# A hybrid attention layer on one core: the query norms of ten heads applied in full, key squares summed in one matmul, and a pair's sums issued at other steps

## The chip, the cores and the metric

The kernel runs on one core of a Trainium2 chip. The metric is device time in microseconds for one execution. A core has a tensor engine (PE, with its weight loads shown apart as PEld), a vector engine (DVE), a scalar engine (ACT), GpSimd (POOL) and a sync engine (SP) that issues DMAs. Each engine works through its own queue in order; semaphores hold an instruction until what it reads is there.

## The reference

One layer of a decoder trunk on 512 tokens of 2048 numbers. After an RMS norm, one wide projection gives queries, keys and values of two groups of heads. Eight forgetting heads (FoX) attend causally with a learned decay. Eight NSA query heads share two key groups and attend to compressed, selected and windowed keys. Queries and keys are RMS-normalised per head (QK-norm), which is what the change is about. An output projection, a residual add, and a gated feed-forward layer follow. Cut to what matters here:

```python
def _rms_norm(x, g):
    xf = x.astype(jnp.float32)
    y = xf * lax.rsqrt(jnp.mean(xf * xf, axis=-1, keepdims=True) + RMS_EPS)
    return (y * g.astype(jnp.float32)).astype(x.dtype)

proj = h @ w_in
qf, kf, vf, ff, qn, kc, vc, ks, vs, kw, vw, gt = jnp.split(proj, cuts, axis=-1)
qf = _rms_norm(qf.reshape(B, T, Hf, Dh), fox_q_norm)
kf = _rms_norm(kf.reshape(B, T, Hf, Dh), fox_k_norm)
qn = _rms_norm(qn.reshape(B, T, G, R, Dh), nsa_q_norm)
```

## The kernel before

[...] All matmuls are done in parts: a 32-bit operand is split into a high part (a copy by ACT that rounds) and a low part (what is left, by DVE), and three products of parts stand for one. `split2` (lines 208 to 216) does this for activations, `split_w` (236) for weight tiles `wp`, of which there are two buffers.

The program has these stretches. Up to 60 us a first projection runs. From 60 to 440 the rest of the plain projections is woven with the eight NSA heads and forgetting head 0. From 440 to about 652 six `pair` projections (query and key of forgetting heads 2 to 7 together) and two `vpair` projections run as a form with seven products in place of eight, each product 24 matmuls of 256 columns. Then the output projection, gate and up, and down follow; the change doesn't touch them.

What sets the order: `stagger` (269) runs the projections one after another; each yields `POST` when its matmuls are done, and what is left of it (the norm) is then advanced as "late steps", one at every second step of the next projection from step 7 on (step 4 in the pair stretch, `LAG7`). `weave` (285) puts the attention of the heads between these steps; in the pair stretch `attend` (1149) does so by the table `SPANS`. On top of this a scheduler orders each engine's instructions, so the built order counts more than the written one.

There are two ways to normalise a query or key before the change:

- `normed` (471) is for keys. It scales the projection by the token's factor `rstd` on DVE (`scaled`, 389), squares it in two halves, adds them, splits the sum's 64 rows into `fr`, and forms the sums with one matmul, `ones` as weights and `fr` moving (484), so that every partition holds every token's sum. Then `rsqrt` (319) and one `scalar_tensor_tensor` (488) give the normalised tile, which is split into two parts.
- `query` (454) is for queries. It splits the raw projection times the gain at once, and forms the sums as columns, one number for each token, with four small matmuls in which `fr` is the weight and `ones[:, :2]` moves (`square_sums`, 423, the matmul on 431). `factors` (434) makes a factor `qs` of each row of the scores, and its inverse, in eight small ops. The head's scores are then multiplied by `qs` on DVE as they leave PSUM (604), its biases `nb` are divided by it on POOL (822, 851), and its compressed scores are scaled by it on ACT (607).

In a `pair` (1087) the query goes the second way: squares of the query (1095), one late step; then the key's squares (1098), the copies `fr_q` (inside `square_sums`), a late step, the sums `ss_q` (431) and the copies of the key's squares, two full tiles `fr`; a late step; the key's sums `ss_k` with two matmuls (1105); a late step; the factors, the key's norm and its split.

`fox(h)` (843) is a forgetting head: scores, softmax, four scalings of p on ACT (617), transposes pT on PE (633), their split (`pt`), and products with the values. `nsa(h)` (815) is an NSA head.

Of the kernel before, what the change touches and what calls it, by code (L numbers as in the profile page):

```python
# [12 lines left out]
OP = mybir.AluOpType  # L13
# [70 lines left out]
def hybrid_layer(ctx: ExitStack, tc: tile.TileContext, xT, vec, ffb, wfg, wfirst, win, cmpw, wout, wos, wgu, wdn, out):  # L84
# [279 lines left out]

    gains = ap_.tile([P, 6], F32, name="gains")
    nc.vector.tensor_scalar_mul(gains, vt[:, 0:6], -0.5 / HD)
    for i in (V_FQ, V_NQ):
        nc.vector.tensor_scalar_mul(gains[:, i:i + 1], vt[:, i:i + 1], -SCALE)
# [84 lines left out]

    def query(name, gain, kept):

        z = yield from proj(name, True)
        r = place()
        if kept:
            t = ftile(f"t_{name}")
            nc.scalar.activation(t, z, AF.Copy, scale=gain)  # L460
        else:
            split2(r, z, gain)
        sq = squares(name, z)
        yield POST
        o = yield from square_sums(name, sq, "m")
        if kept:
            split2(r, t)
        yield
        live[name] = r, *factors(name, o)

    def normed(name, gain, tag, bufs=5):
# [16 lines left out]
        nc.vector.scalar_tensor_tensor(t, t, gain, y, op0=OP.mult, op1=OP.mult)  # L488
        if tag == "ox":
            r = [loose(f"{name}{p}") for p in range(2)]  # L490
        else:
            r = ap_.tile([P, KV], FR, tag=tag, name=name, bufs=bufs)
            if name[:2] == "ks":
                with_compressed[name] = r[:, :64 + T]
                if name == "ks1":
                    nc.scalar.activation(r[:, :64], Kc1.bitcast(F32), AF.Copy)
            r = r[:, 64:64 + 2 * T].rearrange("p (s t) -> p s t", s=2)

            first_keys[name] = r[:, :, :P]
            r = [r[:, p] for p in range(2)]  # L500
# [63 lines left out]
    class Branch:  # L564


        def __init__(self, name, q, k, v, nbs, gcol, apart=False, first_keys=None):
            self.kc = None
            q, self.qs, _ = q
            self.name, self.q, self.k, self.v, self.nbs, self.gcol, self.apart = name, q, k, v, nbs, gcol, apart  # L570
            self.first_keys = first_keys

        def scores(self):
# [3 lines left out]
            for i in reversed(range(NB)):  # L577
# [20 lines left out]
                else:  # L598
# [4 lines left out]
                    nb = pi  # L603
                nc.vector.tensor_tensor_reduce(pi, s[:, :n], nb, self.qs[:, i:i + 1], 3e38, OP.add, OP.min, st[:, 0, i:i + 1])
                if self.kc is not None and i < NB - 1:
                    for n, at in ((i, 0), (NB - 1, 64 + P))[:1 + (i == 0)]:
                        nc.scalar.activation(self.into[:, n, :64], b[:, at:at + 64], AF.Copy, scale=self.qs[:, n:n + 1])
                nc.scalar.activation(pi, pi, AF.Exp, scale=-1.0, bias=st[:, 0, i:i + 1], accum_out=st[:, 1, i:i + 1])
# [206 lines left out]
    def nsa(h):  # L815
        g = h // 4
        q = live.pop(f"qn{h}")

        def nbs(i):
            n = P * (i + 1)  # L820
            nb = ap_.tile([P, T], F32, tag="nb", name=f"nb{h}{i}", bufs=2)
            nc.gpsimd.tensor_scalar(nb[:, :n], E[:, T - n:], q[2][:, i:i + 1], 2.0 ** -(h + 1), op0=OP.mult, op1=OP.mult)
            return nb[:, :n]

        o = ps.tile([P, T], F32, tag="o", name=f"on{h}")
        s, w = [Branch(f"{b}{h}", q, live[f"k{m}{g}"], live[f"v{m}{g}"],
                       nbs, 3 * h + c, b == "w", first_keys.get(f"k{m}{g}"))
                for b, m, c in (("s", "s", 1), ("w", "w", 2))]
# [14 lines left out]
    def fox(h):  # L843
# [4 lines left out]
        def nbs(i):  # L848
            n = P * (i + 1)
            nb = ap_.tile([P, T], F32, tag="nb", name=f"nbf{h}{i}", bufs=2)  # L850
            nc.gpsimd.tensor_scalar(nb[:, :n], ck[:, :n], ncq[:, i, h:h + 1], q[2][:, i:i + 1], op0=OP.add, op1=OP.mult)
            nc.gpsimd.affine_select(nb[:, n - P:n], nb[:, n - P:n], pattern=[[-1, P]], compare_op=OP.is_ge,
                                    fill=BIG, base=0, channel_multiplier=1)
            return nb[:, :n]
# [19 lines left out]
    def nsa_q(h):  # L874
        return query(f"qn{h}", gain(V_NQ), h < 2)

# [210 lines left out]
    def pair(h):  # L1087
# [8 lines left out]
        yield  # L1096
        ks = ftile(f"sq_{k}")
        nc.scalar.activation(ks, t, AF.Square)
        oq = yield from square_sums(q, sq, "t", 2)
        fr = [ap_.tile([P, T], FR, tag=tag, name=f"fr_{k}{tag}") for tag in ("fr", "sb")]  # L1100
        split2(fr, ks)
        yield
        ok = ps.tile([P, T], F32, tag="t", name=f"ss_{k}", bufs=2)
        for p in range(2):
            nc.tensor.matmul(ok, ones, fr[p], start=(p == 0), stop=(p == 1))
        yield
# [928 lines left out]
```

## Time and profile before

| What | us |
|---|---|
| Median of three runs | 2093.97 (2092.68 to 2099.3) |
| The profiled execution | 2096.57 |
| Its span on the core | 2094.8 |

| Stretch of the span, us | PE idle, us | What runs |
|---|---|---|
| 0 to 60 | 1.1 | first projection |
| 60 to 440 | 3.9 | projections, NSA heads, forgetting heads 0 and 1 |
| 440 to 660 | 15.0 | pairs, forgetting heads |
| 660 to 832 | 2.8 | output projection |
| 832 to 2095 | 4.6 | gate, up, down |

The idle times are a stretch's length less PE's busy time in it. PE is busy nearly throughout, and a busy PE need not be at full speed: the granted clock is a column of its own. Two views read alike but differ: the table of waits names the engine whose instruction ended last before PE went on, while the timeline rows of that engine tell what that instruction had waited for itself.

### The profile page before, as it was taken

How to read it: one execution, taken by the hardware profiler on the slowest of the kernel's cores; microseconds unless marked ns; L12 is line 12 of the kernel's file. 1: busy time of each engine (PE TensorE's matmuls, PEld its weight loads, DVE VectorE, ACT ScalarE, POOL GpSimd, SP SyncE). 2: the span in 40 equal slices, each digit the busy share in tenths (PEclk: the TensorE clock that was granted, in tenths of full speed). 3: DMA queues.
4: the chain of work that ended last, by engine and by line, in shares of the span. 5: the costliest groups of instructions: out<-in, count | busy, mean ns of one | idle time of the engine just before them, and what ended most of it. 6: DMA issues, size and time to landing. Idle time of an engine off the chain costs nothing.

```text
span 2094.8 us, 40209 instructions
## 1 busy us (share of the span) xinstructions
PE 2067.6 (99%) x16219; PEld 1984.4 (95%) x16219; DVE 1785.5 (85%) x2738; ACT 1069.1 (51%) x1420; POOL 360.8 (17%) x545
## 2 busy tenths in 40 slices
PE   9999999999999999999999999999999999999999
PEld 8888988899998898999999999999999999999999
DVE  6677678887777877999999999999999987889898
ACT  6556565666666545534444343343433455565554
POOL 1043454522121011111111111111111000000000
PEclk9999999999999999999999999999999999999999
DMA  5685776966675575576776777777777797579865
GB/s 210 207 181 164 177 169 176 217 199 177 208 184 181 177 250 180 165 209 184 195 191 189 204 184 181 209 183 197 193 185 202 239 332 260 153 237 329 299 176 150
DMA packets 142155, 424.24 MB, mean 203 GB/s; under 512 B 17608, under 2 KB 17608, under 8 KB 141968
## 3 DMA queue, kind: packets, MB, share of 16 engines
q1 hardware_dynamic: 91168, 289.21, 41.4%
q0 software_dynamic: 44176, 106.19, 25.8%
q10 hardware_dynamic: 6624, 26.27, 3.3%
q8 instruction: 127, 2.08, 0.4%
q14 instruction: 60, 0.49, 0.1%
HBM read 389.34 MB, written 124.53 MB: 245 GB/s over the span
## 4 chain that ended last, share of the span: by engine, by line
PE 88%; DVE 5%; ACT 3%; issue 2%; DMA 1%; POOL 0%; DVEq 0%; ACTq 0%; SPq 0%; POOLq 0%
PE q L1780 40%; PE pd L1919 13%; PE pd L1924 7%; PE ps_kf L1061 3%; PE po L1370 2%; PE ps_vs L544 2%; PE ps_qn L259 1%; PE po L261 1%; PE ps_vf L544 1%; PE ps_qn L261 1%; PE ps_qn L260 1%; PE po L259 1%; PE po L260 1%; PE ps_vf L1061 1%; PE ps_first L261 1%
## 5 line engine op out<-in xcount | busy, mean ns | idle before, releaser
L95 ACT ACTIVATE bigm<-r 128x1792 fp32r<-128x1792 f32 x174 | 298.2, 1714 | 454.6 <-PE q L1780 320.0
L92 DVE TENSOR_TENSOR bigm<-r,bigm 128x1792 fp32r<-128x1792 f32 x174 | 351.4, 2019 | 5.8 <-ACT bigm L95 5.2
L92 DVE TENSOR_TENSOR r<-r 128x512 f32<-128x512 f32 x522 | 267.2, 512 | 34.5 <-DMA r<-wgu 22.3
L141 POOL DMA_DIRECT2D wsum<-wdn x176 | 120.4, 691 | 700.9 <-ACT bigm L95 602.8
L1780 PE MATMUL q<-bigm 128*128 128x256 f32 x1848 | 217.0, 276 | 0.0
L1780 PE MATMUL q<-formy,bigm 128*128 128x256 f32 x1848 | 216.8, 276 | 0.0
L1780 PE MATMUL q<-forma,bigm 128*128 128x256 f32 x1848 | 216.8, 276 | 0.0
L1780 PE MATMUL q<-formx,bigm 128*128 128x256 f32 x1848 | 216.8, 276 | 0.0
L1780 PEld LDWEIGHTS q<-bigm 128*128 128x128 f32 x1848 | 213.1, 188 | 0.0
L1780 PEld LDWEIGHTS q<-forma,bigm 128*128 128x128 f32 x1848 | 213.0, 188 | 0.1
L1780 PEld LDWEIGHTS q<-formy,bigm 128*128 128x128 f32 x1848 | 212.9, 188 | 0.1
L1780 PEld LDWEIGHTS q<-formx,bigm 128*128 128x128 f32 x1848 | 212.9, 188 | 0.0
L1919 PE MATMUL pd<-bigm 128*128 128x256 f32 x1200 | 146.9, 276 | 0.0
L1919 PEld LDWEIGHTS pd<-bigm 128*128 128x128 f32 x1200 | 141.0, 188 | 0.0
L92 DVE TENSOR_TENSOR bigm<-wd,bigm 128x1024 fp32r<-128x1024 f32 (+1 forms) x62 | 107.8, 1738 | 12.5 <-ACT bigm L95 12.3
L95 ACT ACTIVATE bigm<-rawm 128x768 fp32r<-128x768 f32 (+2 forms) x72 | 66.0, 927 | 98.9 <-PE pd L1924 64.3
L95 ACT ACTIVATE bigm<-wd 128x1024 fp32r<-128x1024 f32 (+1 forms) x62 | 91.1, 1469 | 9.8 <-DVE wd L92 6.1
L92 DVE TENSOR_TENSOR bigm<-rawm,bigm 128x768 fp32r<-128x768 f32 (+2 forms) x72 | 75.5, 1058 | 23.8 <-ACT bigm L95 23.0
L1924 PE MATMUL pd<-bigm 128*128 128x256 f32 x600 | 80.7, 276 | 0.0
L1061 PE MATMUL ps_kf<-bigm,wp_kf 128*128 128x256 f32 x576 | 79.7, 290 | 0.3 <-DVE wp_kf L92 0.3
L1061 PEld LDWEIGHTS ps_kf<-bigm,wp_kf 128*128 128x128 f32 x576 | 74.6, 197 | 1.1 <-DVE wp_kf L92 0.5
L141 POOL DMA_DIRECT2D fsump<-win x72 | 49.1, 751 | 150.6 <-ACT wp_ks L95 39.5
(626 smaller groups left out, 4373.4 us busy)
## 6 DMA issues: line engine op xcount, KB each, us to landing
r<-wgu SPq DMA_DIRECT2D x174, 512.0 KB, 4.3
wsum<-wdn POOLq DMA_DIRECT2D x176, 256.0 KB, 5.1
rawm<-ad SPq DMA_DIRECT2D x44, 512.0 KB, 6.7
wd<-wdn SPq DMA_DIRECT2D x40, 512.0 KB, 6.0
wd<-wsum SPq DMA_DIRECT2D x40, 512.0 KB, 7.0
ad<-cb ACTq DMA_DIRECT2D x22, 896.0 KB, 6.5
fsump<-win POOLq DMA_DIRECT2D x72, 256.0 KB, 5.8
rawm<-ad SPq DMA_DIRECT2D x44, 384.0 KB, 3.6
```

The costliest lines, as they stand in the source:

```text
L92: return pin(nc.vector.tensor_tensor(*args, op=op))
L95: return pin(nc.scalar.activation(*args, **kw))
L141: d = nc.gpsimd.dma_start(step[0], step[1], **step[2])
L259: nc.tensor.matmul(o, lh, rh, start=start, stop=False)
L260: nc.tensor.matmul(o, lh, rl, start=False, stop=False)
L261: nc.tensor.matmul(o, ll, rh, start=False, stop=stop)
L544: nc.tensor.matmul(z[2 * b + t][:, :cols[n]], x[:, xp, at], wp[n][kk], start=(c == 0 and kk == 0 and n == 0 and (t == 0 or gcols is not No ...
L1061: nc.tensor.matmul(z, w[wp][:, u * P:(u + 1) * P], form(f, u)[xp], start=(fresh and m == 0), stop=(m == len(todo) - 1), skip_group_check=True)
L1370: nc.tensor.matmul(q[b][:, h * 256:(h + 1) * 256], w[wp][:, u * P:(u + 1) * P], a[xp], start=(h == 0 and u == 0 and wp == 0 and xp == 0), ...
L1780: nc.tensor.matmul(o, w[wp][:, fb, cs], a[:, xp, fa], start=(k == 0 and h == 0 and wp == 0 and xp == 0), stop=(g == NG - 1 and kk == 1 and ...
L1919: nc.tensor.matmul(b[q][k][:, h * 256:(h + 1) * 256], w[0][:, fb, q * P:(q + 1) * P], a[xp][:, fa], start=(j == 0 and h == 0 and xp == 0), ...
L1924: nc.tensor.matmul(b[q][k][:, h * 256:(h + 1) * 256], w[1][:, fb, q * P:(q + 1) * P], a[0][:, fa], start=False, stop=(j == NJ - 1), skip_g ...
```

## The change

It has two parts.

First, the queries of the eight NSA heads and of forgetting heads 0 and 1 are normalised by `normed`, as keys are, with the gains of queries folded into the columns of `gains`. `query` is gone. These queries have no row factors, so an NSA head's bias is one POOL op per head (E times the head's slope) where eight were, the compressed scores of the first block and the last are copied by one ACT op, and scores leave PSUM with a factor of 1.0.

Second, in a `pair` the key's squares are formed in two halves that are added (`squares(k, t)`), so that the sum is one matmul over one tile `fr`. The copies of the query's squares come a late step ahead of the key's squares, the query's sums one late step later than before, the key's sums, the factors and the key's norm two late steps later. Forgetting heads 2 to 7 keep row factors.

```diff
+    gains = ap_.tile([P, 7], F32, name="gains")
+    nc.vector.tensor_scalar_mul(gains[:, 0:6], vt[:, 0:6], -0.5 / HD)
+    V_FQ_WHOLE = 6
+    nc.vector.tensor_scalar_mul(gains[:, 6:7], gains[:, V_FQ:V_FQ + 1], -SCALE)
+    nc.vector.tensor_scalar_mul(gains[:, V_NQ:V_NQ + 1], gains[:, V_NQ:V_NQ + 1], -SCALE)
...
-    def query(name, gain, kept):
-
-        z = yield from proj(name, True)
-        r = place()
-        if kept:
-            t = ftile(f"t_{name}")
-            nc.scalar.activation(t, z, AF.Copy, scale=gain)
-        else:
-            split2(r, z, gain)
-        sq = squares(name, z)
-        yield POST
-        o = yield from square_sums(name, sq, "m")
-        if kept:
-            split2(r, t)
-        yield
-        live[name] = r, *factors(name, o)
...
         nc.vector.scalar_tensor_tensor(t, t, gain, y, op0=OP.mult, op1=OP.mult)
-        if tag == "ox":
+        if tag == "q":
+            r = place()
+        elif tag == "ox":
...
-                nc.vector.tensor_tensor_reduce(pi, s[:, :n], nb, self.qs[:, i:i + 1], 3e38, OP.add, OP.min, st[:, 0, i:i + 1])
+                nc.vector.tensor_tensor_reduce(pi, s[:, :n], nb, 1.0 if self.qs is None else self.qs[:, i:i + 1], 3e38, OP.add, OP.min, st[:, 0, i:i + 1])
...
-        def nbs(i):
-            n = P * (i + 1)
-            nb = ap_.tile([P, T], F32, tag="nb", name=f"nb{h}{i}", bufs=2)
-            nc.gpsimd.tensor_scalar(nb[:, :n], E[:, T - n:], q[2][:, i:i + 1], 2.0 ** -(h + 1), op0=OP.mult, op1=OP.mult)
-            return nb[:, :n]
-
+        nb = ap_.tile([P, T], F32, tag="nb", name=f"nb{h}", bufs=2)
+        nc.gpsimd.tensor_scalar(nb, E, 2.0 ** -(h + 1), 0.0, op0=OP.mult, op1=OP.add)
...
     def nsa_q(h):
-        return query(f"qn{h}", gain(V_NQ), h < 2)
+        return normed(f"qn{h}", gain(V_NQ), "q", 2)
...
     def qf(h):
-        return query(f"qf{h}", gain(V_FQ), False)
+        return normed(f"qf{h}", gain(V_FQ_WHOLE), "q", 2)
...
         sq = squares(q, z)
         yield
-        ks = ftile(f"sq_{k}")
-        nc.scalar.activation(ks, t, AF.Square)
-        oq = yield from square_sums(q, sq, "t", 2)
-        fr = [ap_.tile([P, T], FR, tag=tag, name=f"fr_{k}{tag}") for tag in ("fr", "sb")]
-        split2(fr, ks)
+        oq = square_sums(q, sq, "t", 2)
+        next(oq)
+        yield
+        sq = squares(k, t)
+        yield
+        oq = yield from oq
+        fr = ap_.tile([P, T], FR, tag="fr", name=f"fr_{k}")
+        split2([fr[half], fr[second_half]], sq[half])
+        yield
         yield
         ok = ps.tile([P, T], F32, tag="t", name=f"ss_{k}", bufs=2)
-        for p in range(2):
-            nc.tensor.matmul(ok, ones, fr[p], start=(p == 0), stop=(p == 1))
+        nc.tensor.matmul(ok, ones, fr, start=True, stop=True)
         yield
```

How the built order moves shows at two places. The first is pair 4, where its late steps stand among the products of the next projection (`ps_vf`, whose weight tiles are `wp_vf_1`, `wp_vf_2`, ...) and the transposes `pT_f` of forgetting head 3. PE's rows before:

```order
L1061 MATMUL ps_vf_6075<-f_7_4640,wp_vf_1_6070 128x256
L431 MATMUL ss_qf_6104<-ones,fr_qf_6103 128x2 x4
L633 MATMUL pT_f_6141<-ident,p_f_5964 128x128 x2
L1061 MATMUL ps_vf_6027<-bigm,wp_vf_2_6114 128x256 x12
L633 MATMUL pT_f_6141<-ident,p_f_5964 128x128 x2
L1061 MATMUL ps_vf_6027<-bigm,wp_vf_2_6114 128x256 x6
L1105 MATMUL ss_kf_6154<-fr_kf4fr,ones 128x512
L1061 MATMUL ps_vf_6027<-bigm,wp_vf_2_6114 128x256 x3
L1105 MATMUL ss_kf_6154<-fr_kf4sb,ones 128x512
```

PE's rows of the changed kernel at the same place:

```order
L1049 MATMUL ps_vf_5934<-f_7_4499,wp_vf_1_5929 128x256
L625 MATMUL pT_f_5995<-ident,p_f_5823 128x128 x4
L434 MATMUL ss_qf_5961<-ones,fr_qf_5960 128x2 x4
L1049 MATMUL ps_vf_5886<-bigm,wp_vf_2_5971 128x256 x24
L625 MATMUL pT_f_6022<-ident,p_f_5823 128x128 x4
L1049 MATMUL ps_vf_5934<-bigm,wp_vf_3_6029 128x256 x12
L625 MATMUL pT_f_6046<-ident,p_f_5823 128x128 x2
L1049 MATMUL ps_vf_5934<-bigm,wp_vf_3_6029 128x256 x6
L1096 MATMUL ss_kf_6057<-fr_kf_6012,ones 128x512
```

All four transposes now stand ahead of the query's sums, the next product runs unbroken, and the key's single sum has moved from that product into the one behind it. ACT's rows there before, from the query's squares on (`L617` scales p_f):

```order
L418 ACTIVATE sq_qf_6084<-t_qf_5666 64x512
L617 ACTIVATE p_f_5964<-p_f_5964,st_f_5965 128x512
L617 ACTIVATE p_f_5964<-p_f_5964,st_f_5965 128x384
L617 ACTIVATE p_f_5964<-p_f_5964,st_f_5965 128x256
L617 ACTIVATE p_f_5964<-p_f_5964,st_f_5965 128x128
L1098 ACTIVATE sq_kf_6101<-t_kf_5665 128x512
L95 ACTIVATE fr_qf_6103<-sq_qf_6084 64x512
L95 ACTIVATE wp_vf_2_6114<-ws_pair_1_5920 128x1024
L95 ACTIVATE wp_vf_3_6171<-ws_pair_3_5956 128x1024
L95 ACTIVATE fr_kf4fr<-sq_kf_6101 128x512
```

and in the changed kernel, from the last scaling of p_f on:

```order
L609 ACTIVATE p_f_5823<-p_f_5823,st_f_5824 128x128
L95 ACTIVATE fr_qf_5960<-sq_qf_5943 64x512
L95 ACTIVATE wp_vf_2_5971<-ws_pair_1_5779 128x1024
L421 ACTIVATE sq_kf_5983<-t_kf_5523 64x512
L422 ACTIVATE sb_kf_5984<-t_kf_5523 64x512
L95 ACTIVATE pt_f_5994<-pT_f_5995 128x512
L95 ACTIVATE wp_vf_3_6029<-ws_pair_3_5815 128x1024
L95 ACTIVATE fr_kf_6012<-sq_kf_5983 64x512
```

The key's squares have left their place ahead of `fr_qf` and stand, as two halves, behind the next weight tile. The second place is DVE at the late steps of forgetting head 0's query, among sums that prepare the pair stretch (`d`, `f`, `acc`) and the split of the weight tile `wp_qf_0`. Before, the small factors `qs_qf`:

```order
L443 TENSOR_TENSOR qs_qf_4471<-qs_qf_4471 128x4
L998 TENSOR_TENSOR f_5_4460<-d_5_4417,f_5_4460 128x256
L444 TENSOR_SCALAR qs_qf_4471<-qs_qf_4471 128x4
L988 TENSOR_TENSOR d_6_4489<-d_6_4489,bigm 128x256
L445 TENSOR_TENSOR qs_qf_4471<-qs_qf_4471 128x4
L998 TENSOR_TENSOR f_5_4461<-acc,f_5_4461 128x256
L446 SCALAR_TENSOR_TENSOR qs_qf_4471<-qs_qf_4471 128x4
L989 TENSOR_TENSOR d_6_4489<-d_6_4489,bigm 128x256
L92 TENSOR_TENSOR wp_qf_0_4513<-ws_qf_0_4511,wp_qf_0_4513 128x1024
```

and in the changed kernel, where the split of `wp_qf_0` stands just ahead of these rows:

```order
L324 SCALAR_TENSOR_TENSOR tmp_qf_4330<-ss_qf_4313,tmp_qf_4330 128x512
L969 TENSOR_TENSOR d_6_4348<-d_6_4348 128x256
L329 SCALAR_TENSOR_TENSOR y_qf_4329<-tmp_qf_4330,y_qf_4329 128x512
L976 TENSOR_TENSOR d_6_4348<-d_6_4348,bigm 128x256
L474 SCALAR_TENSOR_TENSOR t_qf_4245<-t_qf_4245,gains,y_qf_4329 128x512
L977 TENSOR_TENSOR d_6_4348<-d_6_4348,bigm 128x256
L399 TENSOR_TENSOR t_kf_4362<-ps_kf_4259,rstd 128x512
L976 TENSOR_TENSOR acc<-d_6_4348,bigm 128x256
L92 TENSOR_TENSOR qq<-t_qf_4245,qq 128x512
```

Ops of 4 columns became ops of 512 columns, and the query's low part (`qq`) is now made here, at the end of the norm, and not as soon as the projection ends.

More of the change, by code (lines that the diff above doesn't have):

```diff
@@ L363, in hybrid_layer @@
     nc.gpsimd.affine_select(trif, trif, pattern=[[1, T]], compare_op=OP.is_ge, fill=0.0, base=0, channel_multiplier=-1)
-    gains = ap_.tile([P, 6], F32, name="gains")
-    nc.vector.tensor_scalar_mul(gains, vt[:, 0:6], -0.5 / HD)
-    for i in (V_FQ, V_NQ):
+    gains = ap_.tile([P, 7], F32, name="gains")
[3 more added lines that the diff above has]
+    nc.vector.tensor_scalar_mul(gains[:, V_NQ:V_NQ + 1], gains[:, V_NQ:V_NQ + 1], -SCALE)
+    for i in (V_FQ,):
         nc.vector.tensor_scalar_mul(gains[:, i:i + 1], vt[:, i:i + 1], -SCALE)
@@ L568, in __init__ @@
             self.kc = None
-            q, self.qs, _ = q
+            self.qs = None
+            if len(q) == 3:
+                q, self.qs, _ = q
             self.name, self.q, self.k, self.v, self.nbs, self.gcol, self.apart = name, q, k, v, nbs, gcol, apart
@@ L603, in scores @@
                     nb = pi
-                nc.vector.tensor_tensor_reduce(pi, s[:, :n], nb, self.qs[:, i:i + 1], 3e38, OP.add, OP.min, st[:, 0, i:i + 1])
+                nc.vector.tensor_tensor_reduce(pi, s[:, :n], nb, 1.0 if self.qs is None else self.qs[:, i:i + 1], 3e38, OP.add, OP.min, st[:, 0, i:i + 1])
                 if self.kc is not None and i < NB - 1:
-                    for n, at in ((i, 0), (NB - 1, 64 + P))[:1 + (i == 0)]:
-                        nc.scalar.activation(self.into[:, n, :64], b[:, at:at + 64], AF.Copy, scale=self.qs[:, n:n + 1])
+                    if i:
+                        nc.scalar.activation(self.into[:, i, :64], b[:, :64], AF.Copy)
+                    else:
+                        nc.scalar.activation(self.into[:, ::3, :64], b[:, :2 * (64 + P)].rearrange("p (n c) -> p n c", n=2)[:, :, :64], AF.Copy)
                 nc.scalar.activation(pi, pi, AF.Exp, scale=-1.0, bias=st[:, 0, i:i + 1], accum_out=st[:, 1, i:i + 1])
@@ L817, in nsa @@
         q = live.pop(f"qn{h}")
-        def nbs(i):
-            n = P * (i + 1)
-            nb = ap_.tile([P, T], F32, tag="nb", name=f"nb{h}{i}", bufs=2)
-            nc.gpsimd.tensor_scalar(nb[:, :n], E[:, T - n:], q[2][:, i:i + 1], 2.0 ** -(h + 1), op0=OP.mult, op1=OP.mult)
-            return nb[:, :n]
+        nb = ap_.tile([P, T], F32, tag="nb", name=f"nb{h}", bufs=2)
+        nc.gpsimd.tensor_scalar(nb, E, 2.0 ** -(h + 1), 0.0, op0=OP.mult, op1=OP.add)
         o = ps.tile([P, T], F32, tag="o", name=f"on{h}")
         s, w = [Branch(f"{b}{h}", q, live[f"k{m}{g}"], live[f"v{m}{g}"],
-                       nbs, 3 * h + c, b == "w", first_keys.get(f"k{m}{g}"))
+                       lambda i: nb[:, T - P * (i + 1):], 3 * h + c, b == "w", first_keys.get(f"k{m}{g}"))
                 for b, m, c in (("s", "s", 1), ("w", "w", 2))]
@@ L850, in nbs @@
             nb = ap_.tile([P, T], F32, tag="nb", name=f"nbf{h}{i}", bufs=2)
-            nc.gpsimd.tensor_scalar(nb[:, :n], ck[:, :n], ncq[:, i, h:h + 1], q[2][:, i:i + 1], op0=OP.add, op1=OP.mult)
+            nc.gpsimd.tensor_scalar(nb[:, :n], ck[:, :n], ncq[:, i, h:h + 1], q[2][:, i:i + 1] if len(q) == 3 else 1.0, op0=OP.add, op1=OP.mult)
             nc.gpsimd.affine_select(nb[:, n - P:n], nb[:, n - P:n], pattern=[[-1, P]], compare_op=OP.is_ge,
```

## The prediction

> **What bounds the kernel now.** I read the busy times on the profile's first page first, then the table of busy time by stretch of the span, then what the tensor engine waited for in each stretch, and last the timelines of the three busiest engines around one of the longest waits.
>
> ```profile
> span 2094.8 us, 40209 instructions
> PE 2067.6 (99%) x16219; PEld 1984.4 (95%) x16219; DVE 1785.5 (85%) x2738; ACT 1069.1 (51%) x1420; POOL 360.8 (17%) x545
> ```
>
> PE is busy for all but 27.2 us of the span, so the kernel gains only by giving PE less to do, by closing holes out of those 27 us, or by letting it run at a higher clock. The table by stretch says where the holes are (columns: stretch, length, busy us of PE, PEld, DVE, ACT, POOL with counts, granted clock, DMA share, GB/s).
>
> ```profile
> 60.00:440.00 380.00, 376.13 (x2273) 329.55 (x2272) 284.08 (x717) 216.33 (x492) 150.01 (x216) 1.00 0.72 183
> 440.00:660.00 220.00, 205.03 (x1605) 198.47 (x1605) 170.30 (x322) 150.60 (x276) 51.37 (x82) 0.97 0.70 203
> 832.00:2095.00 1263.00, 1258.37 (x11090) 1258.11 (x11088) 1158.53 (x1449) 579.42 (x488) 135.58 (x199) 1.00 0.73 210
> ```
>
> The change touches nothing behind 664 us. Ahead of it, PE is idle 3.9 us in the stretch of the projections and the NSA heads (60 to 440), and 15 us in the stretch of the pairs (440 to 660). What PE waited for there:
>
> ```profile
> PE ss_qf L431 <- DVE fr_qf L92: 12.7, 6, 3.0
> PE pT_f L633 <- DVE pt_f L92: 1.5, 4, 0.5
> ```
>
> Six waits of the sums of a query's squares, one for each pair, are 12.7 of the 15 us. Two of them are short, and their timeline rows (start, duration, the wait in brackets) are:
>
> ```profile
> 470.10 0.58 PE L431 MATMUL ss_qf<-ones,fr_qf 128*128 128x2 f32 x4 [0.67 <-DVE fr_qf L92]
> 470.54 1.39 PE L1061 MATMUL ps_kf<-bigm,wp_kf 128*128 128x256 f32 x10
> 577.69 0.58 PE L431 MATMUL ss_qf<-ones,fr_qf 128*128 128x2 f32 x4 [0.36 <-DVE fr_qf L92]
> ```
>
> These are pairs 2 and 5. The other four (pairs 3, 4, 6, 7) share 12.7 - 0.67 - 0.36 = 11.7 us, 2.9 us each. Pair 4 stands for them; first PE, then ACT, then the one DVE row that matters.
>
> ```profile
> 527.49 0.61 PE L431 MATMUL ss_qf<-ones,fr_qf 128*128 128x2 f32 x4 [2.87 <-DVE fr_qf L92]
> 527.96 0.44 PE L633 MATMUL pT_f<-ident,p_f 128*128 128x128 f32 x2
> 528.15 1.62 PE L1061 MATMUL ps_vf<-bigm,wp_vf 128*128 128x256 f32 x12
> ```
>
> ```profile
> 523.16 0.62 ACT L418 ACTIVATE sq_qf<-t_qf 64x512 f32<-64x512 f32 x1
> 523.76 1.92 ACT L617 ACTIVATE p_f<-p_f,st_f 128x512 f32<-128x512 f32 x4
> 525.58 0.61 ACT L1098 ACTIVATE sq_kf<-t_kf 128x512 f32<-128x512 f32 x1
> 526.10 0.61 ACT L95 ACTIVATE fr_qf<-sq_qf 64x512 fp32r<-64x512 f32 x1
> 526.62 1.99 ACT L95 ACTIVATE wp_vf<-ws_pair 128x1024 fp32r<-128x1024 f32 x2
> ```
>
> ```profile
> 526.75 0.69 DVE L92 TENSOR_TENSOR fr_qf<-sq_qf,fr_qf 64x512 fp32r<-64x512 f32 x1 [1.67 <-ACT fr_qf L95]
> ```
>
> PE stopped at 527.49 - 2.87 = 524.62. DVE had nothing to do for 1.67 us, ACT worked without a gap: the square of the whole key tile (L1098) and, ahead of it, four scalings of p_f stand before the copy fr_qf. The bound here is **ACT's queue**, not DVE, which is named only because its op came last.
>
> **The four long waits after the change.** ACT's order becomes sq_qf, the four scalings, fr_qf, wp_2; the key's squares come behind it. So fr_qf starts where sq_kf started, at 525.58 and not at 526.10, 0.52 us earlier. From ACT's start of fr_qf to PE's ss_qf it takes 527.49 - 526.10 = 1.39 us, so ss_qf can run at 526.97. On PE the four transposes pT_f now stand ahead of ss_qf, where two stood behind it and two inside the product. They need only p_f, which ACT ends at 523.76 + 1.92 = 525.68; two cost 528.15 - 527.96 = 0.19 us, four 0.38. So PE idles from 524.62 to about 525.7, transposes until 526.1, idles until 526.97, and starts the product after the four ss matmuls (527.96 - 527.49 = 0.47) at 527.44. Before, the product started at 528.15 with two transposes still to come, which is 528.34 in like terms. Gain **0.90 us a pair**. About 1.9 us of idle time stays, now in two pieces.
>
> The key's sum is one matmul where two stood:
>
> ```profile
> 472.77 0.39 PE L1105 MATMUL ss_kf<-fr_kf2sb,ones 128*128 128x512 f32 x1
> 473.00 0.75 PE L1061 MATMUL ps_kf<-bigm,wp_kf 128*128 128x256 f32 x5
> ```
>
> One costs PE 473.00 - 472.77 = 0.23 us, so 4 x (0.90 + 0.23) = **-4.5 us**. ACT pays one more half-tile square per pair (0.62 by the sq_qf row) and DVE one more add of the same 64x512 shape as the fr_qf row (0.69). They stand behind wp_2, while PE works through a product of 24 matmuls (twice the 1.62 for 12, some 3 us), which hides them. Without that cover wp_3 would be late by the 1.3 us of both. The factors and the finished keys come two late steps later; the head that needs them starts a product later still, so I cost this at nothing.
>
> **Pairs 2 and 5.** No transposes stand there; ss_qf moves some ten matmuls of the product down, which take some 1.2 us (the row at 470.54 has 1.39 for ten with the tail of the last). Both waits (0.67, 0.36) are shorter than that, so they go, and each pair saves one matmul: -(0.67 + 0.36 + 2 x 0.23) = **-1.5 us**.
>
> **The clock.** Behind three of the four long waits the granted clock falls:
>
> ```profile
> 496.00:500.00 4.00, 4.00 (x20) 4.00 (x21) 3.04 (x4) 1.80 (x5) 0.82 (x1) 0.50 0.62 88
> 500.00:504.00 4.00, 4.00 (x25) 3.86 (x25) 1.58 (x6) 1.87 (x3) 0.00 (x0) 0.72 0.65 242
> 528.00:532.00 4.00, 4.00 (x32) 3.76 (x33) 3.71 (x6) 2.48 (x7) 1.35 (x2) 1.00 0.60 95
> 604.00:608.00 4.00, 4.00 (x23) 4.00 (x24) 3.34 (x5) 2.17 (x6) 0.83 (x1) 0.58 0.51 75
> 636.00:640.00 4.00, 4.00 (x23) 3.86 (x23) 2.45 (x5) 1.17 (x3) 0.00 (x0) 0.65 0.91 305
> ```
>
> It is 0.50 and 0.72 behind pair 3, 0.58 behind pair 6 and 0.65 behind pair 7, while pair 4 (528 to 532) keeps 1.00 after a wait of the same length. The missing clock is 4 x (0.50 + 0.28 + 0.42 + 0.35) = 6.2 us of PE's work at most. At the low clock not everything takes twice as long: the same twelve matmuls that took 1.62 at pair 4 took 2.91 at pair 3,
>
> ```profile
> 496.83 2.91 PE L1061 MATMUL ps_kf<-bigm,wp_kf 128*128 128x256 f32 x12
> ```
>
> a factor of 1.8, so I take 0.8 x 6.2 = **-5.0 us** if the drops go, with bounds of 0 and 6.2. I expect them to go: they need a nearly empty stretch of about 3 us (one case in four survives even that), and after the change the idle time is 1.1 and 0.9 us with work between. The Trainium skill ("TensorE: Matmul & The Clock Gate", Part 1, What's actually happening) says that the clock halves after at least one idle window of about 3.4 us that runs freely against the kernel. By that rule none of these waits, all under 3.0 us, could halve it; the rows here contradict the length, and the measurement decides. By the rule the term would be 0 and not -5.0; its free phase would explain why pair 4 escaped.
>
> **Queries of the NSA heads and of forgetting heads 0 and 1.** PE issues one 512-wide sum (0.23) for four small ones (470.54 - 470.10 = 0.44): 10 x -0.21 = **-2.1 us**. DVE is what pays:
>
> ```profile
> L396 DVE TENSOR_TENSOR t_kw<-ps_kw,rstd x2: 685/688/692, 105.9 to 187.1; 128x512 f32<-128x512 f32 x2
> L478 DVE TENSOR_TENSOR sb_kw<-t_kw x2: 687/687/687, 106.6 to 187.8; 64x512 f32<-64x512 f32 x2
> 114.83 0.69 DVE L324 SCALAR_TENSOR_TENSOR tmp_kw<-ss_kw,tmp_kw 128x512 f32<-128x512 f32 x1 [0.59 <-ACT tmp_kw L323]
> 115.55 0.69 DVE L329 SCALAR_TENSOR_TENSOR y_kw<-tmp_kw,y_kw 128x512 f32<-128x512 f32 x1
> 116.28 0.75 DVE L488 SCALAR_TENSOR_TENSOR t_kw<-t_kw,gains,y_kw 128x512 f32<-128x512 f32 x1
> 117.73 0.69 DVE L92 TENSOR_TENSOR kw<-t_kw,kw 128x512 fp32r<-128x512 f32 x1 [0.70 <-ACT kw L95]
> L215 DVE SCALAR_TENSOR_TENSOR qq<-ps_qn,gains,qq x6: 732/750/751, 169.4 to 328.3; 128x512 fp32r<-128x512 f32 x6
> L443 DVE TENSOR_TENSOR qs_qn<-qs_qn x8: 150/154/164, 128.8 to 342.2; 128x4 f32<-128x4 f32 x8
> ```
>
> A query treated as a key runs the first six rows, 4.20 us, and drops one L215 (0.75) and five small ops like L443 (0.77): +2.7 us each, +27 for ten. ACT gains at most two full tiles a query, 1.2 us by the 0.61 of fr_qf, and is busy 216 of 380 us. POOL does the opposite: its bias ops
>
> ```profile
> L822 POOL TENSOR_SCALAR nb<-E,qs_qn x64: 375/690/1597, 129.8 to 368.1; 128x512 f32<-128x512 f32 x16, 128x384 f32<-128x384 f32 x16, 128x256 f32<-128x256 f32 x16, 128x128 f32<-128x128 f32 x16
> ```
>
> fall from 64 to 8, so some 56 x 0.69 = 39 us of POOL work go, and scores no longer wait for a bias. DVE has 380 - 284 = 96 us free in this stretch, so most of the 27 fits. Not everywhere:
>
> ```profile
> 388.00:428.00 40.00, 39.13 (x235) 34.55 (x235) 38.68 (x87) 26.33 (x56) 24.62 (x31) 1.00 0.93 239
> ```
>
> Here DVE is 97% busy already, and both forgetting queries (2 x 2.7) fall into it; the form sums in this stretch can slip to later, the weight splits cannot. Bounds: -1 (PE's present waits for ACT and the biases shrink) to +10.8 (four queries in full). I take **+1.5**, near the low end, because PE now idles just 0.9 us in that stretch with DVE as full as it is.
>
> **The end of the stretch.** The scores of the last head (7) stand some 3.5 us later on PE, in
>
> ```profile
> 640.00:664.00 24.00, 23.32 (x161) 21.12 (x160) 23.31 (x46) 21.16 (x41) 5.90 (x8) 1.00 0.65 212
> ```
>
> where DVE is 97% busy. The price lies between 0 and 3.5; I take **+1**, since output weights follow that PE can work on meanwhile.
>
> **Sum.** -4.5 - 1.5 - 5.0 - 2.1 + 1.5 + 1.0 = -10.6 us. The profiled execution took 2096.57 us (its span of 2094.8 and 1.8 around it), which gives 2086.0; it is 2.6 above the median of the three runs (2093.97), which gives 2083.4. I say **2084**, nearer to the median.
>
> **Rivals.**
> - *The clock still drops* (0.20). Two idle pieces with 0.4 us of transposes between them are still a thin stretch of 2.5 us, and what the clock reacts to isn't in the profile. For it: drops came after waits of just under 3 us, so the limit isn't known. Against it: two pieces of about 1 us are far from it. The clock term vanishes: 2084 + 5 = 2089. The same time would follow from the rule of the Trainium skill named above, for another reason.
> - *The waits only change hands* (0.09). ACT is busy without a gap before fr_qf, and wp_2, the key's squares, pt_f and wp_3 follow; if a weight split comes late by what ss_qf comes early, only PE's saved matmuls stay, 2.1 + 6 x 0.23 = 3.5: 2090.5. Against it: PE has a product's 3 us to hide those ops.
> - *DVE becomes the bound in the NSA stretch* (0.06), the slower side. PE works on one split weight tile while the next is split. A tile feeds 24 matmuls of 512 at 0.23, 5.5 us, its split on DVE takes 1.2, so a lag under 4.3 us is absorbed. One query adds 2.7, two close together 5.4. If lags pile up so that most queries are paid in full, 8 x 2.7 = 22 comes on top: 2106. It decides once six or more queries are paid in full. Against it: 96 us of free DVE time.
> - *More than forecast* (0.05): DVE runs smoother without the 56 POOL ops, and the waits at the end don't come: about 2076.
>
> **Chances.** The forecast holds 0.60, with 2079 to 2088 of its own. About 0.3% (6.3 us) is what a measurement of this kernel can tell from no change, so faster means under 2087.7. Faster: 0.57 of the forecast, 0.05, and 0.06 of the first rival, 0.68. Same: 0.03 + 0.14 + 0.09 = 0.26. Slower: 0.06. The range is 2076 to 2096: it takes in the first two rivals and the unknown costs, and leaves out DVE as the bound.
>
> **What would show it.** Right: the waits at ss_qf under 1.2 us in four pairs and gone in two, with a wait at pT_f of about 1 us ahead of each; the granted clock at 1.00 from 490 to 650; PE's waits in 60 to 440 still under 6 us. Wrong: a clock under 0.9 behind a pair (first rival); new waits of PE for wp in the product after ss_qf (second); more than 10 us of waits for DVE before 440 (third), or PE idle for over 2 us between 640 and 664.

## The result, and the profile after

The changed kernel takes 2084.11 us (median of 6 runs, 2082.14 to 2087.26); the kernel before, timed beside it, 2095.97 us (6 runs, 2092.68 to 2099.3). The ratio is 0.9944 with a 95% interval of 0.9929 to 0.9959: faster by 11.9 us. The prediction was 2084. One execution of fill_after and one of dve_double, both below, took 1.7% longer than the others of their kernel and are left out of their medians.

The first lines of the changed kernel's profile, and its busy times by stretch (columns as before: stretch, length, busy us of PE, PEld, DVE, ACT, POOL, granted clock, DMA share, GB/s):

```profile
span 2080.4 us, 40019 instructions
PE 2059.1 (99%) x16183; PEld 1975.4 (95%) x16183; DVE 1809.5 (87%) x2745; ACT 1072.5 (52%) x1406; POOL 327.6 (16%) x489
```

```profile
60.00:440.00 380.00, 375.76 (x2266) 329.21 (x2265) 306.94 (x721) 219.57 (x474) 113.87 (x162) 1.00 0.72 183
440.00:660.00 220.00, 211.61 (x1650) 202.68 (x1650) 180.27 (x337) 156.97 (x288) 54.93 (x81) 0.99 0.70 205
```

PE's idle time in the pair stretch falls from 15.0 to 8.4 us. DVE has 23 us more to do between 60 and 440 and POOL 36 us less. What PE waits for in the pair stretch now:

```profile
PE pT_f L625 <- ACT p_f L609: 4.3, 4, 1.1
PE ss_qf L434 <- DVE fr_qf L92: 2.3, 4, 0.6
```

12.7 us in six waits became 6.6 us in eight, two in each of four pairs. Pair 4 again, PE first, then ACT (start, duration, row; the wait in brackets):

```profile
517.07 0.65 PE L625 MATMUL pT_f<-ident,p_f 128*128 128x128 f32 x4 [1.12 <-ACT p_f L609]
518.31 0.61 PE L434 MATMUL ss_qf<-ones,fr_qf 128*128 128x2 f32 x4 [0.59 <-DVE fr_qf L92]
518.77 3.07 PE L1049 MATMUL ps_vf<-bigm,wp_vf 128*128 128x256 f32 x24
```

```profile
515.09 1.92 ACT L609 ACTIVATE p_f<-p_f,st_f 128x512 f32<-128x512 f32 x4
516.91 0.62 ACT L95 ACTIVATE fr_qf<-sq_qf 64x512 fp32r<-64x512 f32 x1
517.43 1.04 ACT L95 ACTIVATE wp_vf<-ws_pair 128x1024 fp32r<-128x1024 f32 x1
```

PE stops at 517.07 - 1.12 = 515.95. fr_qf follows the scalings at once, and ss_qf runs 2.36 us after PE's stop, where it was 2.87. The clock drops once, behind pair 6, where it dropped behind three pairs; behind pair 3 (492 to 496) it now stays up:

```profile
492.00:496.00 4.00, 4.00 (x36) 4.00 (x36) 3.97 (x5) 3.87 (x7) 0.34 (x1) 1.00 0.74 142
592.00:596.00 4.00, 4.00 (x21) 4.00 (x22) 3.29 (x5) 3.39 (x7) 0.81 (x1) 0.57 0.49 54
```

So 4 x 0.43 = 1.7 us of clock are missing in this execution. By stretches of 2 us the profiled execution of the kernel before lacked 6.8 us, that is four times 1.7: two lengths of about 3.4 us at half clock behind pair 3, one each behind pairs 6 and 7. These two numbers belong to one execution each. The mean granted clock is on record for every execution, to three places: 0.998 or 0.999 in the six of the changed kernel (0.9983 on average, 3.5 us missing) and 0.994 to 0.998 in the 56 of the kernel before that were timed with the experiments (0.9965 on average, 7.3 us missing). The profiled execution of the changed kernel is its fastest, and it lost less clock than is usual.

A second yardstick helps below. The time from the first matmul of the pairs to the end of the span leaves out what the NSA stretch does: 2094.8 - 439.0 = 1655.8 before, 2080.4 - 435.4 = 1645.0 after. Of the 14.4 us between the two profiles, 10.8 arise from the pairs on and 3.6 ahead of them.

### The profile page after: what moved, and what is told of

Read it like the earlier page. It is cut to its first block, busy times and chain, and to the rows that moved or that the text cites. A ratio compares the mean times of both kernels' runs of the same rounds, so it can differ in the third digit from the quotient of the medians.

```text
span 2080.4 us, 40019 instructions
## 1 busy us (share of the span) xinstructions
PE 2059.1 (99%) x16183; PEld 1975.4 (95%) x16183; DVE 1809.5 (87%) x2745; ACT 1072.5 (52%) x1406; POOL 327.6 (16%) x489
## 4 chain that ended last, share of the span: by engine, by line
PE 87%; DVE 7%; ACT 3%; issue 2%; DMA 1%; POOL 0%; ACTq 0%; DVEq 0%; POOLq 0%
PE q L1771 39%; PE pd L1910 13%; PE pd L1915 7%; PE ps_kf L1049 4%; PE ps_vs L532 2%; PE po L1361 2%; PE ps_vf L532 2%; PE ps_qn L259 1%; PE ps_qn L260 1%; PE ps_qn L261 1%; PE po L261 1%; PE po L259 1%; PE po L260 1%; PE ps_vf L1049 1%; PE ps_first L261 1%
## 5 line engine op out<-in xcount | busy, mean ns | idle before, releaser
L1910 PEld LDWEIGHTS pd<-bigm 128*128 128x128 f32 x1200 | 141.0, 188 | 0.0
L1915 PEld LDWEIGHTS pd<-bigm 128*128 128x128 f32 x600 | 74.3, 188 | 0.0
```

The source lines that it names most:

```text
L1910: nc.tensor.matmul(b[q][k][:, h * 256:(h + 1) * 256], w[0][:, fb, q * P:(q + 1) * P], a[xp][:, fa], start=(j == 0 and h == 0 and xp == 0), ...
L1915: nc.tensor.matmul(b[q][k][:, h * 256:(h + 1) * 256], w[1][:, fb, q * P:(q + 1) * P], a[0][:, fa], start=False, stop=(j == NJ - 1), skip_g ...
```

## The experiments

Each was timed in turns with the kernel before on the same chip; the medians of the kernel before in these sets lie between 2095.7 and 2098.1.

**queries_only** is the first part of the change alone.

```diff
     def pair(h):
...
-        oq = square_sums(q, sq, "t", 2)
-        next(oq)
-        yield
-        sq = squares(k, t)
+        ks = ftile(f"sq_{k}")
+        nc.scalar.activation(ks, t, AF.Square)
+        oq = yield from square_sums(q, sq, "t", 2)
...
```

> First part alone (norm applied to ten queries, pairs as before). My account: the pairs start about 2.8 us earlier than before (439.0 in the profile of before, 435.4 in that of the change, of which 0.8 come from ahead of 60 us), the six waits at ss_qf stay near 12.7 us, the clock still drops behind some of them; about 2 to 3 us faster. Rival (more work on DVE costs in this stretch what PE saves, and the shift seen is chance): 0 to 1 us, and over 4 us of waits for DVE ahead of 440.

Measured: 2095.15 us beside 2096.97, ratio 0.9991 (0.9982 to 1.0), so 1.8 us at the edge of what can be told. The pairs start at 436.8; from there to the end it takes 1656.3, as before. The six waits are as they were, and the clock drops behind all four long ones, this time behind pair 4 too:

```profile
PE ss_qf L434 <- DVE fr_qf L92: 12.5, 6, 3.0
```

```profile
524.00:528.00 4.00, 3.94 (x21) 3.94 (x22) 3.05 (x5) 2.21 (x6) 1.39 (x2) 0.58 0.46 56
```

**pairs_only** is the second part alone.

```diff
     def nsa_q(h):
-        return normed(f"qn{h}", gain(V_NQ), "q", 2)
+        return query(f"qn{h}", gain(V_NQ), h < 2)
...
     def qf(h):
-        return normed(f"qf{h}", gain(V_FQ_WHOLE), "q", 2)
+        return query(f"qf{h}", gain(V_FQ), False)
```

> Second part alone (queries of NSA heads and forgetting heads 0 and 1 as before). My account: 8 to 11 us faster; the waits at pT_f and ss_qf are together 1.7 us in each of four pairs and gone in two, and fewer clock drops than before (one or none where there were three). Rival (parts need each other, because row factors hold up POOL or ACT): under 6 us.

Measured: 2085.05 beside 2096.97, ratio 0.9941 (0.9929 to 0.9954), 11.9 us faster; from the pairs on 1644.3. Nearly the whole gain of the change is here. Its profile has the waits of the change, and one clock drop.

**steps_only** keeps the new late steps but squares and sums the key in the old way.

```diff
         oq = square_sums(q, sq, "t", 2)
         next(oq)
         yield
-        sq = squares(k, t)
+        ks = ftile(f"sq_{k}")
+        nc.scalar.activation(ks, t, AF.Square)
         yield
         oq = yield from oq
-        fr = ap_.tile([P, T], FR, tag="fr", name=f"fr_{k}")
-        split2([fr[half], fr[second_half]], sq[half])
+        fr = [ap_.tile([P, T], FR, tag=tag, name=f"fr_{k}{tag}") for tag in ("fr", "sb")]
+        split2(fr, ks)
...
```

> Late steps of the pair as changed, but the key's squares in one full tile and two matmuls as before. My account: ACT's order is what pays, so all but 1.4 us (six matmuls of 0.23) of pairs_only: 7 to 10 us faster, the same waits as pairs_only. Rival (the single matmul and the shorter copies pay, because ACT and DVE are what the pairs wait for): 3 us or less.

Measured: 2085.39, ratio 0.9942 (0.993 to 0.9955), 11.6 us faster; from the pairs on 1644.4. So the single matmul, together with the halves that it needs, is worth 0.3 us and not 1.4; the runs of the two kernels lie in the same range (2084.3 to 2086.1 and 2084.5 to 2086.1). In the profile of pairs_only the last matmul of the pairs' products starts 1.1 us earlier than in steps_only (641.6 against 642.7), and near it a wait stands that steps_only doesn't have; its row in the table of waits:

```profile
PE s_f L259 <- ACT kf L95: 0.8, 1, 0.8
```

**halves_only** does the opposite: halves and one matmul, at the old late steps.

```diff
         sq = squares(q, z)
         yield
-        ks = ftile(f"sq_{k}")
-        nc.scalar.activation(ks, t, AF.Square)
+        ks = squares(k, t)
         oq = yield from square_sums(q, sq, "t", 2)
-        fr = [ap_.tile([P, T], FR, tag=tag, name=f"fr_{k}{tag}") for tag in ("fr", "sb")]
-        split2(fr, ks)
+        fr = ap_.tile([P, T], FR, tag="fr", name=f"fr_{k}")
+        split2([fr[half], fr[second_half]], ks[half])
...
```

> The kernel before, with the key's squares in two halves and one matmul, but at the old late steps, so that ACT has two half squares ahead of fr_qf where it had one full one. My account (ACT's queue ahead of fr_qf sets the four waits): each of them about 0.6 us longer than before (3.4 to 3.6), six matmuls less (-1.4), clock drops behind all four: 0 to 3 us slower than before. Rival (the single matmul is what pays): 1 us or more faster, waits as before.

Measured: 2100.8 beside 2095.74, ratio 1.0021 (1.0012 to 1.003), slower by more than was expected (in its profile only by 1.8 from the pairs on). The clock accounts for most of the difference: the profiled execution is the fastest of ten, with a mean clock of 0.996, and the other nine have 0.995 (10 us missing), where the kernel before beside it has 0.9965 on average (7.4 us). The waits are 16.3 us in six, the longest 3.8, and ACT's rows at pair 4 say why: two squares stand ahead of fr_qf.

```profile
524.80 0.61 ACT L418 ACTIVATE sq_kf<-t_kf 64x512 f32<-64x512 f32 x1
525.44 0.63 ACT L419 ACTIVATE sb_kf<-t_kf 64x512 f32<-64x512 f32 x1
526.09 0.63 ACT L95 ACTIVATE fr_qf<-sq_qf 64x512 fp32r<-64x512 f32 x1
```

The kernel before, pairs_only, steps_only and halves_only agree: what stands ahead of fr_qf in ACT's queue sets the time, and the single matmul doesn't. How much of that time is the wait itself and how much the clock that falls behind it, the next run helps to separate.

**fill_before** puts useless work into the waits of the kernel before.

```diff
-        o = ps.tile([P, NB, 2], F32, tag=tag, name=f"ss_{name}", bufs=bufs)
+        whole = ps.tile([P, T], F32, tag=tag, name=f"ss_{name}", bufs=bufs)
+        o = whole[:, :2 * NB].rearrange("p (n c) -> p n c", n=NB)
...
+        if bufs > 1 and name[2:] in "3467":
+            for i in range(22):
+                nc.tensor.matmul(whole[:, 256:], ones, xg[i % 8][:, 0, :256], start=True, stop=True)
         for i in range(NB):
```

> The kernel before, with 22 matmuls of 256 columns on data long there put ahead of ss_qf in pairs 3, 4, 6 and 7, into columns that nobody reads. They fill the wait and take nothing from the path. My account (the clock falls because PE stands empty): granted clock 1.00 behind all four, each wait at ss_qf 0.2 to 0.6 us, and 4 to 6 us faster though nothing useful is done earlier. Rival (the drops have another cause, or the low clock costs nothing that counts): the clock still falls behind two or three of them, 0 to 1 us.

Measured: 2088.97 beside 2096.97, ratio 0.9959 (0.9946 to 0.9971), 8.0 us faster; from the pairs on 1647.7, so 8.1 less. The clock is 1.00 in every stretch of 2 us from 440 to 664; behind pair 3:

```profile
496.00:500.00 4.00, 4.00 (x35) 3.95 (x35) 3.92 (x6) 2.32 (x4) 0.83 (x1) 1.00 0.63 97
```

This settles that the empty time brings the clock down: ss_qf comes no earlier behind the product ahead of it, and PE works more. It also sizes it. The missing clock was 6.8 us, and the waits of pT_f for pt_f (1.5 us before) are gone from this profile; together 8.3, where 8.1 were found. Read alone, this would price a missing microsecond of clock at a whole one. The closer comparison under "The clock" below gives some 0.8, which leaves about 1 us of the 8.1 unaccounted for.

**fill_part** has 10 such matmuls where fill_before has 22.

> The kernel before, with 10 matmuls of 256 columns (1.1 us) in place of the 22 of fill_before ahead of ss_qf in pairs 3, 4, 6 and 7: work, then one wait of about 1.7 us, as long as the two waits of the change together. My account (the clock falls on how empty PE is in some stretch of 3.4 us, and 1.7 us of idle time lies at the edge, as the one drop left in the change shows): one drop or none, 5 to 8 us faster than the kernel before. Rival (any wait over about 1.5 us in one piece makes it fall): three or four drops, within 1.5 us of the kernel before.

Measured: 2088.87 beside 2098.12, ratio 0.9958 (0.9945 to 0.9972), 9.3 us faster (8.4 from the pairs on in the profiles), no drop in the profile. The scheduler moved the four transposes ahead of ss_qf here, so the idle piece that is left is shorter than the expectation had it, and the drop's edge isn't tested as meant:

```profile
496.59 0.61 PE L435 MATMUL ss_qf<-ones,fr_qf 128*128 128x2 f32 x4 [1.10 <-DVE fr_qf L92]
```

One piece of 1.10 us didn't bring the clock down, in any of four pairs.

**fill_after** has 6 such matmuls in the changed kernel, in the second piece of each gap.

> The changed kernel, with 6 matmuls of 256 columns on old data ahead of ss_qf in pairs 3, 4, 6 and 7, into columns that nobody reads. They fill the second piece of the gap (0.6 us) and nothing else. My account (empty PE time makes the clock fall; one drop of 3.4 us at half clock is left, worth 1.7 us): no drop, 1 to 2 us faster than the change. Rival (the drop that is left comes from something else): a drop stays, within 0.5 us.

Measured: 2082.97 (five executions, 2081.35 to 2090.89), ratio to before 0.9942 (0.9927 to 0.9957), which can't be told from the change. In the profile no clock is missing before the end of the span, and the five executions have a mean clock of 0.9994 where those of the change have 0.9983, so the drops do go. From the pairs on the profile takes 1643.6 us where the change takes 1645.0; the 1.4 us fit a drop, but the times don't confirm them. Inconclusive as to the time.

**scale_dve** goes on along the same line: it moves three of the four scalings of p_f from ACT to DVE.

```diff
-                if self.gcol is None:
+                if self.gcol is None and (i == NB - 1 or name[1:] not in "2356"):
                     nc.scalar.activation(pi, pi, AF.Copy, scale=st[:, 2, i:i + 1])
```

> The changed kernel, with three of the four scalings of p_f (384, 256 and 128 columns) on DVE in place of ACT for forgetting heads 2, 3, 5 and 6, those that stand in the four gaps. The built order then has ss_qf 18 matmuls into the next product. My account (ACT's queue is what is left of the waits, and DVE has 1.7 us free there): the wait at pT_f falls from 1.1 to 0.6-0.9 us, that at ss_qf goes, no clock drop is left: 3 to 5 us faster than the change. Rival (DVE is the next bound; its splits come late): waits for wp or pt on DVE take their place, within 1 us of the change.

Measured: 2077.16 us beside 2095.74, ratio 0.9903 (0.989 to 0.9916), 7 us below the change and faster than both kernels. The waits at pT_f and ss_qf are gone, no clock is missing, and from the pairs on it takes 1637.1. PE's rows at pair 4, and the scalings on DVE:

```profile
515.85 0.66 PE L625 MATMUL pT_f<-ident,p_f 128*128 128x128 f32 x4
516.71 2.33 PE L1049 MATMUL ps_vf<-bigm,wp_vf 128*128 128x256 f32 x18 [0.20 <-ACT wp_vf L95]
518.88 0.50 PE L434 MATMUL ss_qf<-ones,fr_qf 128*128 128x2 f32 x4
```

```profile
514.92 0.88 DVE L611 TENSOR_SCALAR p_f<-p_f,st_f 128x384 f32<-128x384 f32 x3
```

Three scalings take DVE 0.88 us, where four take ACT 1.92, so p_f is ready when PE's product ends. The gain was larger than expected because the wait at pT_f went altogether.

**scale_old_queries** is the same without the first part of the change.

> The pairs as changed, three of four scalings on DVE as in scale_dve, but the queries of the NSA heads and of forgetting heads 0 and 1 as before the change. If the two parts are independent, what queries_only showed (1.8 us) is missing: 1 to 3 us slower than scale_dve, all of it ahead of the pairs' start (439 in place of 436.6). Rival (row factors cost nothing once the pairs are smooth): within 0.7 us of scale_dve.

Measured: 2077.04 us, ratio 0.991 (0.9897 to 0.9924). By the medians it is the same as scale_dve and the rival held; by the ratios it is 1.5 us slower, with intervals that overlap, so the times don't decide. The two profiles show the first part's lead and how some of it is lost: the pairs start at 440.0 here and at 436.6 in scale_dve, the span ends at 2075.2 and 2073.7. scale_dve is 3.1 us ahead when the output projection's form of seven products begins (682.5 against 685.6) and 1.8 us when it ends (743.4 against 745.2); in between PE waits in scale_dve for a weight tile, at a place where scale_old_queries has no wait:

```profile
737.31 4.98 PE L1361 MATMUL po<-osums_a,wp_o 128*128 128x256 f32 x40 [1.13 <-ACT wp_o L95]
```

The copy by ACT that ends this wait (736.20) had itself waited for PE's product before it, and two copies near it (728.29 and 738.80) for the load of the weight sums (ws_o). That the loads set the pace there is a reading of one profile and isn't shown.

**dve_double** adds to DVE once more what the change added.

```diff
-        rsqrt(y, o, float(HD), ftile(f"tmp_{name}"), False)
+        tmp = ftile(f"tmp_{name}")
+        rsqrt(y, o, float(HD), tmp, False)
+        for _ in range(4 if tag == "q" else 0):
+            nc.vector.tensor_tensor(tmp, t, y, op=OP.mult)
```

> The changed kernel, with four more ops of 128x512 on DVE in the norm of each of the ten queries (2.7 us each, 27 us in all), which doubles what the change adds to DVE there and lengthens the query's chain as much. Nobody reads what they write. My account (DVE has over 70 us free between 60 and 440 and a query is not wanted at once): 0 to 5 us slower than the change. Rival (DVE became the bound there, so that more of it is paid in full): 15 to 27 us slower.

Measured: 2094.94 us, ratio to before 0.999 (0.998 to 0.9999), 10 to 11 us slower than the change, between the two accounts. The pairs start at 447.5, which is 10.9 us later than the mean of 436.6 in the four profiles with the first part as it is (435.4, 436.8, 436.6, 437.7). So 40% of the added 27 us is paid. From 60 us to the pairs PE is idle for 10.0 us in place of 4.2, in small waits of which these are the longest (the first was 1.8 in the change):

```profile
PE ps_vf L535 <- DVE wp_vf L92: 2.6, 1, 2.6
PE s_f L259 <- DVE st_f L597: 1.1, 1, 1.1
PE ps_qf L261 <- DVE wp_qf L92: 0.9, 1, 0.9
```

Behind the last two the clock is 0.50 from 412.7 to 416.1, a drop that the other profiles don't have there. What the rest of the 10.9 us is made of stays open.

**pool_eight** gives POOL its eight bias ops for each head back.

```diff
-        nb = ap_.tile([P, T], F32, tag="nb", name=f"nb{h}", bufs=2)
-        nc.gpsimd.tensor_scalar(nb, E, 2.0 ** -(h + 1), 0.0, op0=OP.mult, op1=OP.add)
+        def nbs(i):
+            n = P * (i + 1)
+            nb = ap_.tile([P, T], F32, tag="nb", name=f"nb{h}{i}", bufs=2)
+            nc.gpsimd.tensor_scalar(nb[:, :n], E[:, T - n:], 2.0 ** -(h + 1), 0.0, op0=OP.mult, op1=OP.add)
+            return nb[:, :n]
```

> The changed kernel with eight bias ops for each NSA head on POOL, as before the change, but without row factors: some 39 us of POOL work come back between 120 and 370, and nothing waits for a factor. Theory that DVE's added 27 us are hidden in its own free time: within 1.5 us of the change. Rival (they are paid for by POOL's relief, since POOL's ops slow DVE's): 3 to 8 us slower than the change, and the pairs start that much later.

Measured: 2086.09 us, ratio to before 0.9958 (0.9944 to 0.9972), 2.0 us above the change with intervals that overlap. The pairs start at 439.1, 2.5 us later than that mean, and DVE's ops come late twice:

```profile
PE on L260 <- DVE pt_s L92: 1.8, 3, 1.0
PE pT_s L625 <- DVE p_s L611: 0.9, 1, 0.9
```

Again between the two accounts: in these profiles POOL's relief is worth about as much as the first part gains ahead of the pairs. The times don't confirm it, and that POOL's ops slow DVE's is not shown: one of the eight DVE ops `ct<-ct,mc` of 128x128 takes 1.91 us here beside a median of 0.29, but in the kernel before, with as many POOL ops, the longest of them takes 0.29.

## Why the prediction was right, point by point

**The bound** was read rightly. ACT's queue ahead of fr_qf set the four long waits, although the table of waits names DVE. steps_only, halves_only and scale_dve change that queue in three ways, and the time follows each, in part through the clock.

**The four waits.** The forecast had ss_qf 526.97 - 524.62 = 2.35 us behind PE's stop and the product 2.82 behind it; the profile has 2.36 and 518.77 - 515.95 = 2.82. The two pieces were given as 1.1 and 0.9, and are 1.1 and 0.6, since the transposes' last result comes later than the next issue. Not foreseen: the four later waits of pT_f for pt_f (1.5 us) went too; in the built order the copies of the key's squares no longer stand ahead of pt_f's.

**The single matmul** was priced at 6 x 0.23 = 1.4 us and is worth 0.3 by the times. In the profile of pairs_only the saved time meets a key that isn't ready sooner, a wait of 0.8 us; the late finish of the key had been costed at nothing. The profile of the change lacks this wait, so it is not shown to be the whole reason.

**Pairs 2 and 5.** Their waits are gone, as foreseen.

**The clock.** The prediction's factor of 0.8 was right. dve_double and pool_eight have the waits of the change in the pair stretch (4.3 and 2.3 us) but no drop there. From the first matmul of the pairs to the last the change takes 638.0 - 435.4 = 202.6 us, dve_double 648.8 - 447.5 = 201.3 and pool_eight 640.2 - 439.1 = 201.1. So a drop of 1.7 us of missing clock cost 1.3 to 1.5, about 0.8 of it. The term of -5.0 was too large all the same. In the two profiles 6.8 - 1.7 = 5.1 us of clock came back, worth some 4.1; by the means over all executions 7.3 - 3.5 = 3.8 us, worth some 3. Two errors pull against each other: the rows that the term counts miss the edges of the drops (6.2 us where 6.8 were missing), and not all drops go. The two pieces of the change stand in five profiles (after, pairs_only, steps_only, dve_double, pool_eight), and a drop follows 3 of these 20 gaps, each time behind pair 6. The rival in which the clock still drops was right to that extent, and its sign, a clock under 0.9 behind a pair, did show (0.57).

Which gap brings a drop is decided by where it falls on a fixed grid. In the kernel before the drops start at 495.45, 604.68 and 635.40, which are 32 and 9 lengths of 3.413 us apart; in queries_only at 493.91, 524.63, 603.14 and 633.86, which are 9, 23 and 9 lengths apart. PE's busy time in windows of this grid around the four long waits of the kernel before (stretch, length, busy us of PE with its matmuls, granted clock, DMA share, GB/s):

```profile
492.04:495.45 3.41, 0.63 (x6) 1.00 0.35 141
522.76:526.17 3.41, 1.86 (x17) 1.00 0.40 143
526.17:529.58 3.41, 2.09 (x18) 1.00 0.07 2
601.26:604.68 3.42, 1.17 (x10) 1.00 0.20 77
631.98:635.40 3.42, 1.52 (x13) 1.00 0.94 307
```

The wait of pair 4 is cut in two by the edge at 526.17, and no drop follows either half; the waits of pairs 3, 6 and 7 lie mostly in one window, and a drop follows each. In the changed kernel an edge, at 517.07, cuts the gap of pair 4 too, and the gap of pair 6 lies almost whole in one window:

```profile
513.66:517.07 3.41, 2.29 (x22) 1.00 0.72 211
517.07:520.48 3.41, 2.82 (x22) 1.00 0.10 9
588.76:592.17 3.41, 1.81 (x15) 1.00 0.51 103
```

All 15 drops in the traces start at the end of a window in which PE was busy for 0.44 to 1.86 us. The limit isn't sharp in this measure: in halves_only no drop follows a window with 1.50 (600.06 to 603.47). Nor does it say why the first drop in the kernel before lasts two lengths. Where the grid lies against the kernel differs from profile to profile, which fits the spread of the mean clock among executions of one kernel (0.994 to 0.998 before). The Trainium skill ("TensorE: Matmul & The Clock Gate", Part 1, What's actually happening) gives as the rule for a drop at least one idle window of about 3.4 us, which runs freely against the kernel. The window's length and its free run agree with these traces; that it has to be idle doesn't.

**The ten queries.** -2.1 of PE work and +1.5 of waits for DVE made -0.6. The profiles with the first part start the pairs 2.7 us earlier than those without (436.6 on average against 439.3 in seven). The waits were sized about rightly: PE's idle time from 60 us to the pairs is 3.9 us in the kernel before, 4.2 in the change and 5.4 in queries_only. The work term was too small: PE's busy time there falls from 375.1 us to 371.2 and 371.4. The reason given, 96 us of free DVE time, was too easy: dve_double shows that the next 27 us would have cost 11. The rival that makes DVE the bound is a real mechanism that this change stops short of. What the first part is worth in the end is not clear of the noise: 1.8 us by queries_only, 0.9 by the medians of the change and pairs_only, nothing by those of scale_dve and scale_old_queries.

**The end of the stretch** was given 1 us. From the last matmul of the pairs to the last of the output projection the profiles take 831.3 - 654.0 = 177.3 us before and 816.6 - 638.0 = 178.6 after, 1.3 more. Of this 0.6 is a wait of the output projection for t_vf; its waits for weights grow only from 2.8 to 3.0, and the rest stays open.

**The sum**, -10.6, stands against 11.9 by the medians, and 14.4 by the two profiles: 12.4 in the pairs' own stretch (215.0 to 202.6), where the terms made 11.0, and 3.6 ahead of it, less what is given back behind it. That 2084 was met to 0.1 us is luck: the forecast started from a median of three runs (2093.97), which six runs put 2.0 us higher, and the gain was 1.3 us larger.

## What to carry to other kernels

When the table of waits names an engine whose op came last but which had itself been idle, follow that op's own wait back: the queue to shorten is the next one, and the cheapest cure is to move what nobody waits for behind what somebody does. Price an idle gap of PE with the clock that it loses, by filling the gap with useless matmuls: here the useless work alone brought 8 us, most of them the clock's. Look at more than one execution before counting drops. A saving ahead of a later stretch may be given back there, as one pair of profiles here suggests, so time it at the end of the kernel.

## What the runs showed of the hardware that was not expected

Matmuls that compute nothing made a kernel 8.0 us faster (ratio 0.9959, 0.9946 to 0.9971), with 22 of them in each of four waits of 2.9 us. The clock is lost in portions of 3.413 us at half speed, 1.7 us of clock each: 6.8 in the profile before, 1.7 after, none in the pair stretch when the waits are filled. The portions start on a grid of that length, behind windows in which PE was busy for at most 1.86 us, and one cost 1.3 to 1.5 us of time. A wait of 2.87 us that an edge of the grid cut in two (pair 4 before) brought none. Three scalings of 384, 256 and 128 columns took DVE 0.88 us together, where four with one of 512 more took ACT 1.92.
